# Delta rule: output norm and gate once for all chunks behind the convolutions, sums of squares on ScalarE, first mask folded into the decay

## The chip, the cores and the metric

The kernel runs on one core of a Trainium2 chip. The metric is device time in microseconds of one execution of the whole program. The engines are named as the profile names them: PE (matmuls), DVE (vector), ACT (activations), POOL (a second, slower elementwise engine), SP (which issues most DMAs).

## The reference, cut to what matters

The program is a stack of four blocks over 512 tokens of width 1024. The change touches only the first block, in which three branches are computed from one projection of the normed input and merged:

```python
def gated_delta_rule(q, k, v, g, beta):          # 4 heads of 128, chunk by chunk
    g = jnp.cumsum(g, axis=-1)
    ...
    lhs = a_kk + jnp.eye(CHUNK)                  # a_kk: strictly lower, k_beta k^T times decay
    sol = lax.linalg.triangular_solve(lhs, rhs, left_side=True, lower=True, unit_diagonal=True)
    ...
    def step(state, inp):
        v_new = u_c - w_c @ state
        o_c = q_c @ state + a_c @ v_new
        state = state * gl_c + k_c^T @ v_new

def gdn_branch(qkv, gate, a, b, conv_w, a_log, dt_bias, norm_w):
    q, k, v = split(silu(conv(qkv)))
    q = l2_normalize(q) * 128 ** -0.5            # x * rsqrt(sum(x*x) + EPS), per head
    k = l2_normalize(k)
    ...
    o = gated_delta_rule(q, k, v, g, beta)
    o = o * rsqrt(mean(o * o, axis=-1) + EPS) * norm_w     # per head
    return o * silu(gate)

y_a = gdn_branch(...)
y_b = stick_breaking_branch(sb_qkv)
y_c = short_conv_branch(sc_x, sc_b, sc_c, conv_sc_w)       # B * conv3(C * x)
merged = gate0 * (y_a @ w0) + gate1 * (y_b @ w1) + gate2 * (y_c @ w2)
```

## The kernel before, in words

A float32 matrix product is made of three matmuls of split operands (`h,whi`, `h,wlo`): `dense` makes one 128x512 block from 8 steps of 3 matmuls, 24 in all, in a PSUM bank `ps_d`. There are three `ps_d` banks, four `ps_p` banks for the delta rule's products and one `ps_s` bank for its state. Weights come through a stream: a DMA loads `wraw`, ACT makes `whi`, DVE makes `wlo`.

The delta rule (`gdn_core`) works on four chunks of 128 tokens. For each chunk `gdn_chunk_prep` turns k and q into token order on PE (transposes of `qkv` tiles at L534), sums their squares (ACT squares `sq`, DVE reduces into `qk_m`), takes a reciprocal root in some ten tiny DVE instructions (`rq_y`, `rq_a`), scales (`kt`, `qt`), transposes back (`kT`, `qT`, L540), and multiplies k by k and q by k into `pa` and `pq`. `dA` holds the decay times beta; `dA<-ps_p,dA` makes the matrix A of it. The inverse of I + A is then built level by level: a mask `lmask` picks a part of A (on POOL), the first one as `L`, the later ones as `Al`; R is the transpose of L; then six levels follow, each of which is `R,Al` (four matmuls), `E` on DVE, `E,L` (four matmuls), and a copy to the new `R` on ACT, with L transposed on DVE. Each step of a level waits for the one before. `gdn_chunk_step` carries the state: `S,kT`, `X,R`, `vn,kd`, and the outputs `S,qd` with `vn,dT` into `ps_s`. At its end stands the norm of the outputs: square on ACT (`gsq`), reduce and reciprocal root on DVE (`go_m`), the product `on`, four transposes on PE (L681) and four multiplications by the gate into `ya`.

`gdn_core` prepares chunk c+1 before it steps chunk c, so the one's step lies beside the other's levels. Behind `gdn_core` comes `short_conv`: four times three dense blocks (`px`, `pc`, `pb`), whose results go through the four temporaries `t` into a tile `yc`; then `stick_breaking` with the blocks of `sb_vf`. The dense blocks of what comes later in the code fill PE while the delta rule waits. Which of them stand where is fixed when the program is built: a scheduler gives each engine a fixed list of instructions, and each engine works through its list in order and waits where an operand is late. A tile of a tag is taken from a ring of buffers (`slot`): the tag `y` has 8 (before: four `ya`, taken ahead of the first chunk, then four `yc`), the tag `x` has 8 (among them the four gates `sgate`), `t` has 4.

```python
        with self.phase("mix", dict(d=3, p=4, s=1), qkv=12, gl=12, gp=6, gm=6, gs=5, y=8, t=4, tg=1):
```

Of the kernel before, what the change touches and what calls it, by code (L numbers as in the profile page):

```python
# [12 lines left out]
ALU = mybir.AluOpType  # L13
AF = mybir.ActivationFunctionType
AX = mybir.AxisListType

P = 128
# [131 lines left out]
class Kern:  # L149
# [373 lines left out]
    def gdn_chunk_prep(self, c):  # L523

        nc, G = self.nc, self.gdn
        cs = slice(c * P, (c + 1) * P)
        H4 = [P, 4, P]
        v3 = lambda t: t.rearrange("p (h n) -> p h n", h=4)
# [26 lines left out]
        dA = self.slot("gp", name="dA")  # L555
        self.tt(v3(dA), v3(t1), self.mstrict.unsqueeze(1).to_broadcast(H4), ALU.add)
        self.act(dA, dA, AF.Exp, scale=-1.0)
        self.tt(v3(dA), v3(dA), bc(G["beta"]), ALU.mult)
        dT = self.slot("gl", name="dT")
        self.tt(v3(dT), v3(t1), self.minclT.unsqueeze(1).to_broadcast(H4), ALU.add)  # L560
        self.act(dT, dT, AF.Exp)
# [2 lines left out]
        ssq = self.tmp("qk_m", shape=(P, 8))  # L564
        for i, ps in enumerate((pk, pq)):
            sq = self.slot("gs", name="sq")
            self.act(sq, ps, AF.Square)
            nc.vector.tensor_reduce(out=ssq[:, 4 * i:4 * i + 4], in_=v3(sq), axis=AX.X, op=ALU.add)
        self.ts(ssq, ssq, EPS, ALU.add)
        y = self.rsqrt(ssq, (P, 8), "8")  # L570
        self.ts(y[:, 4:8], y[:, 4:8], P ** -0.5, ALU.mult)
# [16 lines left out]
        pa, pq = self.ps("p"), self.ps("p")  # L588
        for h in range(4):
            hs = slice(h * P, (h + 1) * P)  # L590
            self.mm(pa[:, hs], kT[:, hs], kT[:, hs])
            self.mm(pq[:, hs], kT[:, hs], qT[:, hs])
        A, aq = dA, dT
        self.tt(A, pa, dA, ALU.mult)
        self.tt(aq, pq, dT, ALU.mult)

        I4 = self.ident.unsqueeze(1).to_broadcast(H4)
        I2 = self.ident.unsqueeze(1).to_broadcast([P, 2, P])
        v2 = lambda t: t.rearrange("p (h n) -> p h n", h=2)
        mk = lambda l: self.lmask[l - 1].unsqueeze(1).to_broadcast(H4)  # L600
        L = self.slot("gm", name="L")
        self.tt(v3(L), v3(A), mk(1), ALU.mult, nc.gpsimd)
        self.tt(v3(L), I4, v3(L), ALU.subtract)
        R = self.slot("gm", name="R")
        self.nc.vector.transpose(out=R, in_=L)
        for l in range(2, N_LEVELS + 1):
# [3 lines left out]
            R2 = self.slot("gl" if l == N_LEVELS else "gm", name="R")  # L610
            L2 = self.slot("gm", name="L") if l < N_LEVELS else None
            half = [slice(g * 2 * P, g * 2 * P + 2 * P) for g in range(2)]
# [10 lines left out]
            for g, c_ in enumerate(half):  # L623
                self.act(R2[:, c_], product(L, E, g))
                if l < N_LEVELS:
                    if l <= 5:
                        self.nc.vector.transpose(out=L2[:, c_], in_=R2[:, c_])
                    else:
                        nc.vector.tensor_copy(out=L2[:, c_], in_=product(E, L, g))
            L, R = L2, R2  # L630
        return dict(kT=kT, kd=kd, qd=qd, vb=vb, aq=aq, R=R, gl=gl)

    def gdn_chunk_step(self, c, w, S):

        nc, G = self.nc, self.gdn
        H4 = [P, 4, P]
        v3 = lambda t: t.rearrange("p (h n) -> p h n", h=4)
        hs = [slice(h * P, (h + 1) * P) for h in range(4)]
        if S is not None:
            pk = self.ps("s")  # L640
            for h in range(4):
                self.mm(pk[:, hs[h]], w["kT"][:, hs[h]], S[:, hs[h]])
            X = self.slot("gs", name="X")
            self.tt(v3(X), v3(pk), G["beg"][:, c, :].unsqueeze(2).to_broadcast(H4), ALU.mult)
            self.tt(X, w["vb"], X, ALU.subtract)
        else:
            X = w["vb"]
        pv = self.ps("s")
        for h in range(4):
            self.mm(pv[:, hs[h]], w["R"][:, hs[h]], X[:, hs[h]])  # L650
        vn = self.slot("gs", name="vn")
        self.act(vn, pv)
        S2 = None
        if c < 3:
            pS = self.ps("s")
            for h in range(4):
                self.mm(pS[:, hs[h]], w["kd"][:, hs[h]], vn[:, hs[h]])
            S2 = self.slot("gs", name="S")
            if S is None:
                self.act(S2, pS)  # L660
            else:
                Sg = self.slot("gs", name="Sg")
                self.tt(v3(Sg), v3(S), w["gl"].unsqueeze(2).to_broadcast(H4), ALU.mult, nc.gpsimd)
                self.tt(S2, pS, Sg, ALU.add)
        po = self.ps("s")
        for h in range(4):
            if S is not None:
                self.mm(po[:, hs[h]], w["qd"][:, hs[h]], S[:, hs[h]], stop=False)
            self.mm(po[:, hs[h]], w["aq"][:, hs[h]], vn[:, hs[h]], start=(S is None))

        sq = self.slot("tg", name="gsq")
        self.act(sq, po, AF.Square)
        m = self.tmp("go_m", shape=(P, 4))
        nc.vector.tensor_reduce(out=m, in_=v3(sq), axis=AX.X, op=ALU.add)
        self.ts(m, m, 1.0 / P, ALU.mult, EPS, ALU.add)
        ro = self.rsqrt(m, (P, 4))
        on = self.slot("gs", name="on")
        self.tt(v3(on), v3(po), ro.unsqueeze(2).to_broadcast(H4), ALU.mult)
        pt = self.ps("s")
        for h in range(4):  # L680
            nc.tensor.transpose(pt[:, hs[h]], on[:, hs[h]], self.ident)  # L681
        cs = slice(c * P, (c + 1) * P)
        for h in range(4):
            self.stt(self.ya[h][:, cs], pt[:, hs[h]], self.col("gdn_norm"), self.sgate[h][:, cs],
                     ALU.mult, ALU.mult)
        return S2

    def gdn_gate(self):
        self.sgate = []
# [9 lines left out]
    def gdn_core(self):  # L699
        lm = [self.slot("x", name="lmask") for _ in range(2)]  # L700
        for i in range(2):
            n = min(4, N_LEVELS - 4 * i) * P
            self.nc.scalar.dma_start(out=lm[i][:, 0:n], in_=self.ins["lmask"][:, i * T:i * T + n])
        self.lmask = [lm[i // 4][:, (i % 4) * P:(i % 4 + 1) * P] for i in range(N_LEVELS)]
        self.ya = [self.slot("y", name="ya") for _ in range(4)]
        S, w = None, self.gdn_chunk_prep(0)
        for c in range(4):
            nxt = self.gdn_chunk_prep(c + 1) if c < 3 else None
            S = self.gdn_chunk_step(c, w, S)
            w = nxt  # L710
# [1028 lines left out]
    def build(self):  # L1739
        self.load_constants()  # L1740
        with self.phase("mix", dict(d=3, p=4, s=1), qkv=12, gl=12, gp=6, gm=6, gs=5, y=8, t=4, tg=1):
            self.mark("norm0")
            self.first_norm()
            self.mark("gdn_proj")
            self.gdn_project()
            self.gdn_gate()
            self.gdn_decay()
            self.mark("gdn_core")
            self.gdn_core()
            self.mark("sc")  # L1750
            self.short_conv()
            self.mark("sb")
            self.stick_breaking(self.gates())
            self.dump_blocks("ya", self.ya)
            self.dump_blocks("yb", self.yb)
            self.dump_blocks("yc", self.yc)
            self.mark("merge")
            wo, accs, old = self.merge()
            self.mark("post0")
            x, hs = self.post_norm(wo, accs, "norm_mix_post", old, "norm_ffn_pre", keep=False, warm=(10, 8))  # L1760
            self.dump_blocks("x1", x)
        with self.phase("ffn1", dict(d=4, p=2, s=2), f=16, part=8, t=3, sy=7, sz=7, so=2):
            self.mark("ffn1")
            x, hs = self.ffn_relu2(x, hs, "norm_ffn_post", "mix0", self.s5_prepare())
            self.dump_blocks("x2", x)
        with self.phase("s5", dict(d=5, b=1, s=1), ut=3, U=5, matB=2, matE=3, matC=2, matL=2, w=6, rf=2, zz=4, half=8, t=4):
            self.mark("s5")
            x = self.s5_layer(x, hs)
            self.dump_blocks("x3", x)
        with self.phase("ffn2", dict(d=6, s=2), f=22, t=8):  # L1770
            self.mark("ffn2")
            x = self.ffn_swiglu(0, x, "ffn0")
            self.dump_blocks("x4", x)
        with self.phase("mla", dict(d=2, z=2, p=3, s=1), c=10, v=4, os=4, mp=7, pt=8, tm=3, t=4):
            self.mark("mla")
            x = self.mla(x)
            self.dump_blocks("x5", x)
            self.pad(self.sp, 96)
        with self.phase("ffn3", dict(d=6, s=2), f=22, t=8):
            self.mark("ffn3")  # L1780
            self.ffn_swiglu(1, x, "ffn1", last=True)
# [126 lines left out]
```

## Time and profile before

| | |
|---|---|
| median of 3 runs | 2231.46 us (2230.91 to 2231.72) |
| the profiled execution | 2235.85 us, span 2234.1 us |
| granted clock of TensorE, mean | 0.987 |
| busy: PE, DVE, ACT, POOL | 2160.5, 1361.5, 1005.8, 177.4 us |
| the delta rule's stretch of the span | about 113 to 282 us |

The profiled execution takes 4.39 us more than the median, 1.75 us of which lie outside its span. [...] PE is busy in 97% of the span, so what changes its waits and its clock changes the time.

### The profile page before, as it was taken

The numbers are of one execution on the slowest core, as the hardware profiler recorded it, in microseconds if no ns is written. First come the engines' busy times: TensorE is split into PE (matmuls) and PEld (weight loads), VectorE is DVE, ScalarE is ACT, GpSimd is POOL, SyncE is SP. The second block draws the span as 40 slices with busy tenths as digits, with TensorE's granted clock in tenths as the row PEclk, the third lists the DMA queues.
The fourth block names the chain that finished last, engine by engine and source line by source line (L and its number), as shares of the span: only waits on it lengthen the run. The fifth ranks groups of instructions, "written<-read, shape, count | busy, mean of one in ns | idle before, by whom it ended". The sixth has DMA issues, their size and how long they took to land.

```text
span 2234.1 us, 28560 instructions
## 1 busy us (share of the span) xinstructions
PE 2160.5 (97%) x10618; PEld 1794.2 (80%) x10618; DVE 1361.5 (61%) x2569; ACT 1005.8 (45%) x1926; POOL 177.4 (8%) x228
## 2 busy tenths in 40 slices
PE   8998999999999999999879999999999999999999
PEld 7777878888888888888668788888878877888887
DVE  6668756667658656666895554354477665543542
ACT  4443335666445454464224433233368765332331
POOL 4123200112000000000000000000022220000000
PEclk9999999999999999999989999999999999999999
DMA  4210123234523344343763223323221112233222
GB/s 153 90 48 29 43 80 119 95 114 156 174 67 105 125 150 141 132 155 103 237 212 124 85 95 101 97 95 95 92 72 34 48 38 66 95 101 98 95 95 94
DMA packets 83370, 231.57 MB, mean 104 GB/s; under 512 B 9632, under 2 KB 19360, under 8 KB 83232
## 3 DMA queue, kind: packets, MB, share of 16 engines
q1 hardware_dynamic: 74016, 208.60, 28.7%
q10 hardware_dynamic: 9216, 21.16, 2.9%
q8 instruction: 83, 1.36, 0.2%
q14 instruction: 55, 0.45, 0.1%
HBM read 202.46 MB, written 27.26 MB: 103 GB/s over the span
## 4 chain that ended last, share of the span: by engine, by line
PE 84%; DVE 9%; ACT 2%; issue 2%; DMA 2%; POOL 1%; SPq 0%; ACTq 0%; DVEq 0%; POOLq 0%
PE ps_d L250 71%; PE ps_p L282 3%; PE ps_z L250 2%; PE ps_p L250 1%; PE ps_s L1724 1%; DMA s5u<-ut 1%; PE ps_p L1699 1%; PE ps_s L282 1%; DVE wlo L224 1%; PE ps_p L1654 1%; DVE t L224 1%; PE ps_p L868 1%; DVE h L231 1%; DVE s5t L224 1%; ACT sb_e L234 1%
## 5 line engine op out<-in xcount | busy, mean ns | idle before, releaser
L250 PE MATMUL ps_d<-h,whi 128*128 128x512 f32 (+1 forms) x3184 | 1004.9, 393 | 8.9 <-DVE t L224 5.1
L234 ACT ACTIVATE whi<-wraw 128x512 fp32r<-128x512 f32 (+1 forms) x648 | 403.1, 625 | 716.8 <-PE ps_d L250 672.9
L250 PEld LDWEIGHTS ps_d<-h,whi 128*128 128x128 f32 (+1 forms) x3184 | 597.9, 189 | 135.0 <-ACT whi L234 4.0
L224 DVE TENSOR_TENSOR wlo<-wraw,whi 128x512 fp32r<-128x512 f32 x585 | 405.7, 697 | 383.6 <-ACT whi L234 378.1
L250 PE MATMUL ps_d<-h,wlo 128*128 128x512 f32 (+1 forms) x1592 | 626.4, 393 | 4.9 <-DVE wlo L224 4.9
L250 PEld LDWEIGHTS ps_d<-h,wlo 128*128 128x128 f32 (+1 forms) x1592 | 300.3, 189 | 67.6 <-DVE wlo L224 6.6
L250 PE MATMUL ps_d<-fh,whi 128*128 128x512 f32 x608 | 237.3, 390 | 0.0
L250 PE MATMUL ps_d<-fl,whi 128*128 128x512 f32 x608 | 237.0, 390 | 0.0
L250 PE MATMUL ps_d<-fh,wlo 128*128 128x512 f32 x608 | 236.6, 389 | 0.0
L224 DVE TENSOR_TENSOR t<-ps_d,rsb 128x512 f32<-128x512 f32 x136 | 92.9, 688 | 127.2 <-PE ps_d L250 124.3
L250 PEld LDWEIGHTS ps_d<-fl,whi 128*128 128x128 f32 x608 | 114.2, 188 | 23.7
L250 PEld LDWEIGHTS ps_d<-fh,wlo 128*128 128x128 f32 x608 | 114.2, 188 | 23.5
L250 PEld LDWEIGHTS ps_d<-fh,whi 128*128 128x128 f32 x608 | 114.2, 188 | 23.2
L224 POOL TENSOR_TENSOR wlo<-wraw,whi 128x512 fp32r<-128x512 f32 (+3 forms) x63 | 82.4, 1313 | 150.5 <-ACT whi L234 150.4
L234 ACT ACTIVATE fh<-t 128x512 fp32r<-128x512 f32 x76 | 47.9, 631 | 63.1 <-DVE t L224 54.4
L224 DVE TENSOR_TENSOR fl<-t,fh 128x512 fp32r<-128x512 f32 x76 | 52.5, 691 | 32.7 <-ACT fh L234 30.7
L250 PE MATMUL ps_d<-whi,c 128*128 128x256 f32 (+1 forms) x224 | 52.3, 318 | 2.9 <-ACT v L234 2.2
L224 DVE TENSOR_TENSOR x<-ps_d,x 128x512 f32<-128x512 f32 x56 | 38.6, 689 | 24.7 <-PE ps_d L250 24.4
L250 PE MATMUL ps_d<-zh,wlo 128*128 128x512 f32 x128 | 50.5, 394 | 0.9 <-DVE wlo L224 0.9
L250 PE MATMUL ps_d<-zh,whi 128*128 128x512 f32 x128 | 49.7, 401 | 1.5 <-ACT zh L234 0.9
L250 PE MATMUL ps_d<-zl,whi 128*128 128x512 f32 x128 | 49.8, 390 | 0.0
L224 DVE TENSOR_TENSOR acc<-acc,t 128x512 f32<-128x512 f32 x57 | 44.5, 780 | 4.6 <-ACT t L234 3.2
(391 smaller groups left out, 2911.5 us busy)
## 6 DMA issues: line engine op xcount, KB each, us to landing
wraw<-in_w_gu SPq DMA_DIRECT2D x88, 512.0 KB, 3.3
wraw<-in_w_ff SPq DMA_DIRECT2D x64, 512.0 KB, 3.3
wraw<-in_w_dn SPq DMA_DIRECT2D x44, 512.0 KB, 3.4
wraw<-in_w_gates SPq DMA_DIRECT2D x24, 512.0 KB, 3.4
wraw<-in_w_glu SPq DMA_DIRECT2D x16, 512.0 KB, 3.3
wraw<-in_w_sc SPq DMA_DIRECT2D x12, 512.0 KB, 3.4
gsc<-t SPq DMA_DIRECT2D x24, 256.0 KB, 2.0
sg<-gsc SPq DMA_DIRECT2D x24, 256.0 KB, 3.5
```

The lines of the kernel that those rows point to most:

```text
L224: self.note((eng or self.nc.vector).tensor_tensor(out=out, in0=a, in1=b, op=op))
L231: (eng or self.nc.vector).scalar_tensor_tensor(out=out, in0=a, scalar=s, in1=b, op0=op0, op1=op1)
L234: self.note(self.nc.scalar.activation(out, a, fn, **kw))
L250: self.note(self.nc.tensor.matmul(ps, lhsT=a, rhs=b, start=(start and n == 0), stop=(stop and n == 3 * len(ops) - 1), skip_group_check=loose))
L282: self.nc.tensor.matmul(ps, lhsT=lhsT, rhs=rhs, start=start, stop=stop)
L868: self.nc.tensor.matmul(self.sb_at(z, i), lhsT=self.tri if j == i else self.neg, rhs=self.sb_at(s, j), start=False, stop=(j == i and n == ...
L1654: self.nc.tensor.transpose(pt[:96, c * P:(c + 1) * P], src[:, c, l, :], self.ident)
L1699: self.nc.tensor.transpose(pt[:, oo:oo + P], p[bi][:, c0 + j * P:c0 + (j + 1) * P], self.ident)
L1724: self.note(nc.tensor.matmul(po[64 * h:64 * h + 64, 0:256], lhsT=V[j][:, head:head + 64], rhs=pt[h][j // 2][:, j % 2 * 256:j % 2 * 256 + 256],
```

## The change

Three things. The first mask is multiplied into the decay before the product `pa` is there (POOL `L<-dA,lmask` moves ahead of the transposed k; a DVE multiplication `L<-pa,L` takes its place behind `pa`). The sums of squares of k and q are taken by ACT itself, in eight squares of 128x128 with an accumulated output instead of two of 128x512 and two reduces on DVE. And the outputs are only copied from PSUM in each chunk (`yraw`, a tile of the tag `y`); squares, root, transposes and gate are done once for all four chunks in `gdn_finish`, which is called behind `short_conv` and writes into the gate's own tiles.

```diff
@@ gdn_chunk_prep
         self.tt(v3(dA), v3(dA), bc(G["beta"]), ALU.mult)
+        mk = lambda l: self.lmask[l - 1].unsqueeze(1).to_broadcast(H4)
+        L = self.slot("gm", name="L")
+        self.tt(v3(L), v3(dA), mk(1), ALU.mult, nc.gpsimd)
...
             sq = self.slot("gs", name="sq")
-            self.act(sq, ps, AF.Square)
-            nc.vector.tensor_reduce(out=ssq[:, 4 * i:4 * i + 4], in_=v3(sq), axis=AX.X, op=ALU.add)
+            for h in range(4):
+                self.act(sq[:, h * P:(h + 1) * P], ps[:, h * P:(h + 1) * P], AF.Square,
+                         accum_out=ssq[:, 4 * i + h:4 * i + h + 1])
...
         A, aq = dA, dT
+        self.tt(L, pa, L, ALU.mult)
         self.tt(A, pa, dA, ALU.mult)
         self.tt(aq, pq, dT, ALU.mult)
...
-        L = self.slot("gm", name="L")
-        self.tt(v3(L), v3(A), mk(1), ALU.mult, nc.gpsimd)
         self.tt(v3(L), I4, v3(L), ALU.subtract)
@@ gdn_chunk_step
+        y = self.slot("y", name="yraw")
+        self.act(y, po)
+        self.yraw.append(y)
+        return S2
+
+    def gdn_finish(self):
+
+        m = self.tmp("go_m", shape=(P, 16))
         sq = self.slot("tg", name="gsq")
-        self.act(sq, po, AF.Square)
-        m = self.tmp("go_m", shape=(P, 4))
-        nc.vector.tensor_reduce(out=m, in_=v3(sq), axis=AX.X, op=ALU.add)
+        hs = [slice(h * P, (h + 1) * P) for h in range(4)]
+        for c in range(4):
+            for h in range(4):
+                self.act(sq[:, hs[h]], self.yraw[c][:, hs[h]], AF.Square, accum_out=m[:, 4 * c + h:4 * c + h + 1])
         self.ts(m, m, 1.0 / P, ALU.mult, EPS, ALU.add)
-        ro = self.rsqrt(m, (P, 4))
-        on = self.slot("gs", name="on")
-        self.tt(v3(on), v3(po), ro.unsqueeze(2).to_broadcast(H4), ALU.mult)
-        pt = self.ps("s")
+        ro = self.rsqrt(m, (P, 16), "o")
+        for c in range(4):
+            v = self.yraw[c].rearrange("p (h n) -> p h n", h=4)
+            self.tt(v, v, ro[:, 4 * c:4 * c + 4].unsqueeze(2).to_broadcast([P, 4, P]), ALU.mult)
         for h in range(4):
-            nc.tensor.transpose(pt[:, hs[h]], on[:, hs[h]], self.ident)
-        cs = slice(c * P, (c + 1) * P)
-        for h in range(4):
-            self.stt(self.ya[h][:, cs], pt[:, hs[h]], self.col("gdn_norm"), self.sgate[h][:, cs],
-                     ALU.mult, ALU.mult)
-        return S2
+            pt = self.ps("s")
+            for c in range(4):
+                self.nc.tensor.transpose(pt[:, hs[c]], self.yraw[c][:, hs[h]], self.ident)
+            self.stt(self.sgate[h], pt, self.col("gdn_norm"), self.sgate[h], ALU.mult, ALU.mult)
+        self.ya = self.sgate
@@ gdn_core
-        self.ya = [self.slot("y", name="ya") for _ in range(4)]
+        self.yraw = []
@@ build
             self.short_conv()
+            self.gdn_finish()
```

The change also moves instructions in the engines' lists. The first place is PE's list in the levels of the last chunk. Before, dense matmuls (L250) stand between the level's steps:

```order
L282 MATMUL ps_p<-R,Al 128x128 x4
L250 MATMUL ps_d<-h,whi 128x512
L282 MATMUL ps_p<-E,L 128x128 x4
L250 MATMUL ps_d<-h,wlo 128x512
L250 MATMUL ps_d<-h,whi 128x512 x2
L282 MATMUL ps_p<-R,Al 128x128 x4
L250 MATMUL ps_d<-h,wlo 128x512
L250 MATMUL ps_d<-h,whi 128x512 x2
L250 MATMUL ps_d<-h,wlo 128x512
L282 MATMUL ps_p<-E,L 128x128 x4
```

In the changed program the last levels and the step behind them stand in PE's list without a dense matmul, as all six levels of this chunk do:

```order
L282 MATMUL ps_p<-R,Al 128x128 x4
L282 MATMUL ps_p<-E,L 128x128 x2
L282 MATMUL ps_p<-L,E 128x128 x2
L282 MATMUL ps_p<-E,L 128x128 x2
L282 MATMUL ps_p<-L,E 128x128 x2
L282 MATMUL ps_p<-R,Al 128x128 x4
L282 MATMUL ps_p<-E,L 128x128 x4
L282 MATMUL ps_s<-X,R 128x128 x4
```

The first dense matmul behind them, with the semaphores that each waits for, stands right behind the chunk's last output products and waits for DVE:

```order
L282 MATMUL ps_s<-S,qd 128x128
L282 MATMUL ps_s<-vn,dT 128x128
L250 MATMUL ps_d<-h,whi 128x512 [waits DVE_49]
L250 MATMUL ps_d<-h,wlo 128x512
L250 MATMUL ps_d<-h,whi 128x512 x2
```

What moved: 61 dense matmuls that stood ahead of this point now stand behind it; the three blocks that are complete by then lie in the three `ps_d` banks.

The second place is the short convolution's own work on ACT. Before, its first instruction on a `yc` stands between the levels of the second chunk:

```order
L234 ACTIVATE qT<-ps_p 128x512 [waits PE_49,Pool_49]
L234 ACTIVATE whi<-wraw 128x512 [waits PE_49]
L234 ACTIVATE yc<-t,cols 128x512
L234 ACTIVATE R<-ps_p 128x256 [waits PE_49,Activation_49]
L234 ACTIVATE R<-ps_p 128x256 [waits PE_49]
```

In the changed program the first two stand behind the last chunk's `yraw`:

```order
L234 ACTIVATE R<-ps_p 128x256 [waits PE_49] x3
L234 ACTIVATE vn<-ps_s 128x512 [waits PE_49,Pool_49]
L234 ACTIVATE yraw<-ps_s 128x512 [waits PE_49]
L234 ACTIVATE yc<-t,cols 128x512 x2
L234 ACTIVATE gsq,go_m<-yraw 128x128 [waits Activation_49]
```

And DVE's list has the rest of these two convolutions behind the last level, ahead of the instruction that empties a `ps_d` bank (`t<-ps_d`):

```order
L224 TENSOR_TENSOR E<-cst,ps_p 128x256 [waits PE_49]
L231 SCALAR_TENSOR_TENSOR yc<-t,cols,yc 128x511 [waits Activation_49] x2
L231 SCALAR_TENSOR_TENSOR yc<-t,cols,yc 128x510 [waits DVE_49] x2
L224 TENSOR_TENSOR yc<-yc,t 128x512 [waits DVE_49] x2
L224 TENSOR_TENSOR t<-ps_d,rsb_2039 128x512
L228 TENSOR_SCALAR go_m<-go_m 128x16 [waits Activation_49]
```

The four `yc` are taken from the ring of the tag `y` behind the fourth `yraw`, which is taken in the last chunk's step; before, the four `ya` were taken ahead of the first chunk.

## Rows read from the trace of the kernel before

**Rows 1.** The page's chain that ended last: share of the span by engine.
```profile
PE 84%; DVE 9%; ACT 2%; issue 2%; DMA 2%; POOL 1%; SPq 0%; ACTq 0%; DVEq 0%; POOLq 0%
```

**Rows 2.** PE's waits, 100 to 318 us: total, times, longest, in us.
```profile
PE ps_p L282 <- DVE go_m L228: 3.7, 2, 1.9
PE ps_p L282 <- DVE R L605: 3.4, 2, 1.8
```

**Rows 3.** Stretches of the delta rule: length, busy time of each engine, PEclk, DMA.
```profile
119.59:138.76 19.17, 16.53 (x91) 13.50 (x89) 14.71 (x33) 7.95 (x15) 4.84 (x4) 1.00 0.17 55
157.09:176.05 18.96, 15.98 (x101) 13.36 (x100) 17.33 (x42) 8.01 (x15) 4.85 (x4) 1.00 0.09 29
197.02:216.44 19.42, 17.29 (x109) 14.39 (x107) 16.78 (x35) 7.44 (x14) 5.89 (x5) 1.00 0.09 28
236.58:256.68 20.10, 17.80 (x113) 15.00 (x112) 16.24 (x35) 6.92 (x13) 5.90 (x5) 1.00 0.08 27
138.76:157.09 18.33, 18.33 (x134) 16.87 (x135) 10.71 (x25) 5.25 (x13) 6.73 (x5) 1.00 0.10 30
176.05:197.02 20.97, 20.25 (x146) 18.01 (x146) 17.89 (x36) 6.49 (x15) 6.55 (x5) 1.00 0.17 51
216.44:236.58 20.14, 19.89 (x137) 18.25 (x138) 15.50 (x41) 5.86 (x14) 6.36 (x5) 0.92 0.09 27
256.68:281.70 25.02, 24.68 (x169) 22.35 (x170) 19.59 (x46) 7.83 (x17) 6.37 (x5) 0.93 0.18 54
281.70:317.58 35.88, 35.64 (x159) 29.20 (x159) 16.47 (x35) 8.19 (x13) 0.00 (x0) 1.00 0.28 89
```

**Rows 4.** Timeline of the last chunk's first matrices: start, length, engine, instruction, idle before.
```profile
251.46 0.69 DVE L224 TENSOR_TENSOR dA<-ps_p,dA 128x512 f32<-128x512 f32 x1 [1.22 <-PE ps_p L282]
...
252.23 1.30 POOL L224 TENSOR_TENSOR L<-dA,lmask 128x512 f32<-128x512 f32 x1 [1.12 <-DVE dA L224]
...
253.48 1.29 POOL L224 TENSOR_TENSOR Al<-dA,lmask 128x512 f32<-128x512 f32 x1
...
253.56 1.76 DVE L224 TENSOR_TENSOR L<-cst,L 128x512 f32<-128x512 f32 x1 [0.82 <-POOL L L224]
...
255.25 0.67 DVE L674 TENSOR_REDUCE go_m<-gsq 128x4 f32<-128x512 f32 x1
255.84 0.69 DVE L605 STREAM_TRANSPOSE R<-L 128x512 f32<-128x512 f32 x1
...
256.68 1.28 PE L282 MATMUL ps_p<-R,Al 128*128 128x128 f32 x8 [1.86 <-DVE go_m L228]
```

**Rows 5.** Timeline of one level of the first chunk, same columns.
```profile
142.24 1.05 PE L282 MATMUL ps_p<-R,Al 128*128 128x128 f32 x8
...
143.37 1.15 PE L282 MATMUL ps_p<-E,L 128*128 128x128 f32 x8
...
144.11 0.83 ACT L234 ACTIVATE R<-ps_p 128x256 f32<-128x256 f32 x2 [1.98 <-PE ps_p L282]
```

**Rows 6.** ACT: copies and squares in the delta rule by form, then one with an accumulator elsewhere (timeline).
```profile
L234 ACT ACTIVATE R<-ps_p 128x256 f32<-128x256 f32 x48 | 18.5, 385 | 59.9 <-PE ps_p L282 58.8
L234 ACT ACTIVATE sq<-ps_p 128x512 f32<-128x512 f32 x8 | 4.7, 587 | 2.9 <-PE ps_p L534 2.9
```
```profile
1683.29 0.40 ACT L234 ACTIVATE mp<-mp,a_mn 128x128 f32<-128x128 f32 x1
```

**Rows 7.** Short convolution's instructions by form, 112.8 to 318 us: count, busy, mean ns.
```profile
L234 ACT ACTIVATE yc<-t,cols 128x512 f32<-128x512 f32 x4 | 2.9, 719 | 2.8 <-DVE t L224 2.7
L231 DVE SCALAR_TENSOR_TENSOR yc<-t,cols,yc 128x510 f32<-128x510 f32 x4 | 2.9, 718 | 0.0
```

**Rows 8.** Stretches of 2 us around 1130; columns as in rows 3.
```profile
1130.00:1132.00 2.00, 0.00 (x0) 0.03 (x1) 2.00 (x4) 1.42 (x5) 0.00 (x0) 0.50 0.40 111
...
1136.00:1138.00 2.00, 2.00 (x10) 1.90 (x10) 2.00 (x2) 0.00 (x0) 0.00 (x0) 0.50 0.70 201
```

**Rows 9.** Timeline of PE in the stick-breaking stage.
```profile
538.59 0.39 PE L262 MATMUL ps_s<-sb_al,v 128*128 128x256 f32 x1 [1.50 <-DVE sb_al L224]
```

More of the change, by code (lines that the diff above doesn't have):

```diff
@@ L599, in gdn_chunk_prep @@
         v2 = lambda t: t.rearrange("p (h n) -> p h n", h=2)
-        mk = lambda l: self.lmask[l - 1].unsqueeze(1).to_broadcast(H4)
-        L = self.slot("gm", name="L")
-        self.tt(v3(L), v3(A), mk(1), ALU.mult, nc.gpsimd)
         self.tt(v3(L), I4, v3(L), ALU.subtract)
```

## The prediction

> **What bounds the kernel now.** The chain that ended last lies on PE for 84% of the span [rows 1], so a change counts where it alters PE's idle time or PE's clock; work on the other engines counts only through these. I therefore read PE's waits next. In the delta rule the largest are those for the first R of a chunk: four waits of 1.6 to 1.9 us, 7.1 us together [rows 2] (the rows name `go_m` for two of them, an instruction that shares DVE's queue with R; in [rows 4] it is R that PE's `R,Al` follows). Then I cut the stretch at each chunk's first transpose of k and at its first `R,Al` [rows 3]: the first four rows are the preparations up to R, the next four the levels (the last with the chunk's own step), the ninth the dense work behind the delta rule up to the first `sb_vf` transpose. The reader should see that preparation is PE-busy for only 85 to 90%, that levels without a step beside them (the fifth row) are PE-busy throughout, and that two level stretches have a granted clock of 0.92 and 0.93.
>
> Two prices of PE are needed. The ninth row holds 155 dense matmuls and four `on` transposes: 35.88 us less 0.24 idle and 0.45 for the transposes, over 155, is 0.227 us for one dense matmul. The fifth row holds 22 dense matmuls and 56 small products in 18.33 us without idle time: 0.24 us for a small product.
>
> **What the change removes.** PE's own work stays: as many products, 16 output transposes, as many dense matmuls. What can fall is waiting, and what matters is which dense matmuls remain to fill it.
>
> First mask. Before, from `dA<-ps_p,dA` to `R,Al` the chain of [rows 4] is DVE 251.46, POOL 252.23 to 253.53, DVE `L<-cst,L` 253.56 to 255.32, a reduce of `go_m` in between, R from 255.84, PE at 256.68: 5.2 us. `L<-cst,L` reads SBUF alone and takes 1.76 us; it ends 0.55 us behind POOL's `Al`, so I read it as held until POOL is done. After: `L<-pa,L`, `dA` and `dT` 0.60 us apart (as the reduce and R are), POOL's `Al` from 1.34 to 2.63, so `L<-cst,L` held to 3.2, R to 3.85, PE at 3.95. The gain is 1.3 us a chunk on this chain, not POOL's full step with the reduce, because the mask that now runs beside it still holds DVE.
>
> Sums of squares. Before, a 128x512 square takes 0.59 us [rows 6] and a reduce 0.67 [rows 4]. After, four 128x128 squares stand for each; none with an accumulator from PSUM is in the trace. The nearest row, from SBUF, has 0.40 [rows 6]; the lower bound goes on from 512 columns at 0.587 and 256 at 0.385 [rows 6] to 0.28 at 128, an estimate. I take 0.3, since the source in PSUM is nearest to these: eight cost 2.4 us on ACT where two cost 1.2, and two reduces (1.2 us) leave DVE. The path k to `kt` gains little: 0.5, 0.4, 0.25 and 0.7 us for the four chunks, as DVE's tiny root instructions start when ACT's last square is through, and POOL's `L<-dA,lmask` now runs just then. At 0.40 a square this falls by 0.9 us in sum.
>
> [...]
>
> Preparations together. k to `kt` as above (-1.85), and `kt` to `R,Al`: -0.75, -1.9, -0.95 and -1.4 us. The second is largest since the tiny root of `go_m` (ten instructions) no longer stands ahead of `dA`. Sum of the four: **-6.85 us**.
>
> Levels of chunks 0 to 2. Without norm and gate beside them the second and third stretch should go as the first does now: 18.33 us with 22 dense matmuls [rows 3]. The second will have 22, the third 19 and one product more. That is 18.65 and 18.2 against 20.97 and 20.14 (the latter at a granted clock of 0.92, some 1.6 us lost behind its wait for R): **-4.25**, and **-0.2** for the first, which has one dense matmul less.
>
> **What the change adds.** Last chunk's levels. The changed order has no dense matmul among them. The work is 64 products of 0.24 us, 15.4 us, but without filler the chain sets the pace: `R,Al` to `E,L` 1.13 us, 0.74 to the copy of R, 0.42 for its first half and 0.1 to the next `R,Al` [rows 5], 2.39 us a level. Six levels with the extra `L,E` products, X, R and the outputs come to 18.25 us against 25.02 [rows 3]: **-6.75**, nearly all of it the 28 dense matmuls that left (6.4).
>
> Behind it. Dense filling stopped early because three finished blocks sit in the three banks: the fourth `t` can only come free when a `yc` is written, and the `yc` come behind the last `yraw`. So 61 more dense matmuls stand here, 61 x 0.227 = **+13.9**, and 12 more transposes at 0.11, **+1.3**. And the first dense matmul waits, with PE empty, for a list that starts when the outputs are in PSUM: 0.66 us for `yraw` (a 512-wide ACT instruction, 0.59 [rows 6], and the handover), 0.72 for the first `yc` on ACT, then on DVE four multiply-adds, two products and `t<-ps_d` at about 0.65 each (0.72 alone [rows 7], 0.60 in a row [rows 4]): 5.9 us, **+5.9**. Queued behind that instruction on PE is all dense work of the convolutions and of `sb_vf`; nothing else can run. After a wait like this the clock is down: around 1130 us PE had been empty, and the granted clock stayed at 0.50 to 1138 [rows 8], some 6 us of work at half speed, 3 us lost; behind the two shorter waits it was 1.6 and 1.75 us (0.08 of 20.14 and 0.07 of 25.02 [rows 3]). I take **+2.3**, between 1.6 and 3. Short waits for the single `ps_s` bank in `gdn_finish`: **+0.3**.
>
> Later. The gate's tiles now live to the merge, so four of the eight `x` buffers stay taken where the first stick-breaking heads want theirs. PE already waits there, 1.50 us at 538.59 [rows 9]. I take **+1.0**, between 0.3 and 2.
>
> **Sum.** -6.85 - 4.25 - 0.2 - 6.75 + 13.9 + 1.3 + 5.9 + 2.3 + 0.3 + 1.0 = +6.65 us. On the profiled execution's 2235.85 us that is 2242.5; it lies 4.4 us above the median of the runs shown, on which the sum gives **2238.1 us**. Something like 0.2%, 4.5 us, is what a measurement of this kernel can tell from no change, so the forecast is slower, not by much. In short: the waits that the change aims at were filled or short, and the one that it makes has nothing to fill it.
>
> **Rivals.** *It cancels* (no change). What DVE does beside POOL may be held less than I grant, which gives up to 0.65 us a chunk (`L<-cst,L` freed, 3.95 down to 3.3), 2.6 in all, and the clock may lose only 1.6 behind the long wait: 6.65 - 2.6 - 0.7 = +3.35, **2234.8 us**. For it: two of the four waits for R left no loss of clock at all [rows 2, 3]. Against: `L<-cst,L` was held in [rows 4], and it meets the same `Al` now. It decides from 2.2 us of gain on.
>
> *The convolutions are not held* (faster). If the short convolution's work ran among the levels as before, dense matmuls would fill the last chunk, and neither the wait nor the half clock would come. Then the preparations and levels keep their -11.3, the last levels gain the 1.75 us of their lost clock, and later work costs 1: -12.05, **2219.4 us**. The lists of ACT and DVE speak against it; it needs `t<-ps_d` to be done before the last `yraw`, and the list has it behind six instructions that need that `yraw` past. What decides is where that instruction starts.
>
> *The clock falls earlier too* (slower still). The last chunk has no filler from `kt` on, and PE there idles about 1.3 us before R and 0.5 in each level. The waits of up to 1.8 us in the first two chunks left the clock at 1.00 in the levels behind them, the two of up to 1.9 did not [rows 2, 3]. If half clock lasts through three of these levels, each with 1.9 us of work, some 1.4 us a level are lost, and the long wait's loss is 3: 6.65 + 4.2 + 0.7 = 11.5 at the most, half of that beyond the forecast is **2240.5 to 2243 us**.
>
> **How the numbers follow.** Forecast (2236 to 2240.5) 0.48; cancels 0.28; clock 0.15; not held 0.09. The range takes in the cancelling case and the clock's, and leaves out the faster one: 2230.5 to 2245.5. Slower by over 0.2% is the forecast and the clock's case with a little of their edge gone to no change: 0.61; within 0.2% 0.30; faster 0.09.
>
> **What would show it.** Right: in the last chunk's levels, no L250 row on PE between the first `R,Al` and the last output product, at a period near 2.4 us; behind it a wait of some 6 us put down to DVE's `t`, and a clock of 0.50 for some 4 to 6 us; the four waits for R at most 1 us each, with chunk 2 at full clock. Wrong: a wait of under 3 us there, a clock that stays at 1.00 behind it, a path from k to `kt` that is longer than before (then the squares cost over 0.40, or POOL holds more of the root), or a difference behind 320 us that is over 2 us either way.

## The result and the profile after

The changed kernel takes 2248.12 us (median of 4 runs, 2242.35 to 2249.78) against 2231.59: ratio 1.0066, interval 1.0045 to 1.0087, slower. The forecast was slower by 6.65 us, to 2238.1, in a range of 2230.5 to 2245.5. Measured were 16.5 us by these medians and 14.7 by the ratio, some 15 us, and the time lies outside the range. The two profiled executions differ by less, 2240.6 against 2234.1 us of span, but they are not alike in clock: the changed one had a mean granted clock of 0.990, its other three runs 0.986, the one before 0.987. So the parts below are read within the profile, and the totals from the medians.

The page's chain that ended last, which answers to [rows 1], hardly moves:

```profile
PE 85%; DVE 8%; ACT 3%; issue 2%; DMA 1%; POOL 1%; SPq 0%; ACTq 0%; POOLq 0%; DVEq 0%
```

PE's waits from 100 to 330 us, which answer to [rows 2]:

```profile
PE ps_d L250 <- DVE t L224: 5.9, 1, 5.9
PE ps_p L540 <- DVE kt L224: 3.2, 4, 1.4
PE ps_p L282 <- DVE R L607: 2.5, 4, 1.0
...
PE ps_s L282 <- DVE X L224: 1.0, 2, 0.5
```

The waits for R fell from 7.1 to 2.5 us, those for `kt` rose from 0.8 to 3.2, and a new one of 5.9 us stands first. The stretches, cut at the same instructions as in [rows 3] (four preparations, four levels, the dense work behind the wait):

```profile
118.23:136.01 17.78, 15.82 (x88) 12.94 (x86) 14.19 (x31) 8.39 (x28) 4.88 (x4) 1.00 0.19 59
153.94:170.30 16.36, 15.07 (x100) 12.81 (x98) 13.62 (x28) 9.49 (x36) 4.89 (x4) 1.00 0.10 34
188.37:206.21 17.84, 15.99 (x106) 13.59 (x105) 15.98 (x31) 8.91 (x35) 6.36 (x5) 1.00 0.19 60
224.02:241.94 17.92, 15.51 (x103) 12.98 (x102) 15.50 (x31) 9.13 (x35) 6.32 (x5) 1.00 0.18 59
136.01:153.94 17.93, 17.93 (x134) 16.48 (x135) 11.67 (x25) 5.67 (x14) 6.36 (x5) 1.00 0.10 31
170.30:188.37 18.07, 18.07 (x135) 16.63 (x136) 11.59 (x25) 5.24 (x13) 6.38 (x5) 1.00 0.10 30
206.21:224.02 17.81, 17.81 (x134) 16.45 (x134) 10.31 (x23) 5.15 (x13) 6.38 (x5) 1.00 0.01 2
241.94:261.96 20.02, 17.68 (x128) 15.23 (x128) 10.88 (x24) 5.19 (x13) 6.34 (x5) 1.00 0.00 1
267.83:321.11 53.28, 53.28 (x232) 43.72 (x233) 28.76 (x51) 12.20 (x19) 0.00 (x0) 0.96 0.26 85
```

From the first k transpose to the `sb_vf` transposes these are 202.88 us against 197.99, +4.9 (the sum had +5.65 for this stretch). Between the eighth and the ninth row lie the 5.87 us in which PE stands still. The timeline there shows who holds it:

```profile
262.00 0.60 ACT L234 ACTIVATE yraw<-ps_s 128x512 f32<-128x512 f32 x1 [2.14 <-PE ps_s L282]
262.50 1.32 ACT L234 ACTIVATE yc<-t,cols 128x512 f32<-128x512 f32 x2
263.24 2.73 DVE L231 SCALAR_TENSOR_TENSOR yc<-t,cols,yc 128x511 f32<-128x511 f32 x4 [6.03 <-ACT yc L234]
...
265.89 1.28 DVE L224 TENSOR_TENSOR yc<-yc,t 128x512 f32<-128x512 f32 x2
267.10 0.68 DVE L224 TENSOR_TENSOR t<-ps_d,rsb 128x512 f32<-128x512 f32 x1
...
267.83 0.80 PE L250 MATMUL ps_d<-h,whi 128*128 128x512 f32 x1 [5.87 <-DVE t L224]
```

DVE had been idle for 6.03 us when its first `yc` came: the work was not too much, it was late. Stretches of 4 us around it (columns as in [rows 3]) show the clock:

```profile
262.00:266.00 4.00, 0.00 (x0) 0.00 (x0) 2.76 (x5) 2.98 (x11) 0.00 (x0) 0.96 0.00 0
266.00:270.00 4.00, 2.17 (x5) 1.78 (x6) 3.89 (x9) 0.72 (x1) 0.00 (x0) 0.50 0.00 0
270.00:274.00 4.00, 4.00 (x13) 3.13 (x13) 3.79 (x14) 0.63 (x1) 0.00 (x0) 0.68 0.00 0
```

The nine dense matmuls from 268.43 us on take 3.84 us, 0.43 us for one, the nine from 273.33 on 2.06, 0.23 for one. At 0.50 for 2.17 us of work and at 0.68 over 4, the loss is 1.1 + 1.3 = 2.4 us, an estimate from these shares (taken: 2.3).

So the stretch as a whole went as forecast, and the rest of the 15 us lies elsewhere. One view tells where to look: the tile `fh`, the moving operand of the feed-forward blocks from 700 us on, which the change does not touch (count, then shortest, median and longest time in ns; first before, then after):

```profile
L250 PE MATMUL ps_d<-fh,whi x608: 387/389/478, 703.4 to 2229.3; 128*128 128x512 f32 x152
```

```profile
L250 PE MATMUL ps_d<-fh,whi x608: 388/394/481, 707.2 to 2236.0; 128*128 128x512 f32 x152
```

### The profile page after: what moved, and what is told of

Its sections match the earlier page's. It is cut to its first block, busy times and chain, and to the rows that moved or that the text cites. A ratio compares the mean times of both kernels' runs of the same rounds, so it can differ in the third digit from the quotient of the medians.

```text
span 2240.6 us, 28610 instructions
## 1 busy us (share of the span) xinstructions
PE 2163.4 (97%) x10618; PEld 1790.7 (80%) x10618; DVE 1354.4 (60%) x2519; ACT 1013.4 (45%) x2014; POOL 177.3 (8%) x228
## 4 chain that ended last, share of the span: by engine, by line
PE 85%; DVE 8%; ACT 3%; issue 2%; DMA 1%; POOL 1%; SPq 0%; ACTq 0%; POOLq 0%; DVEq 0%
PE ps_d L250 72%; PE ps_p L282 3%; PE ps_z L250 2%; PE ps_p L250 1%; PE ps_s L1733 1%; PE ps_p L1708 1%; PE ps_s L282 1%; PE ps_p L1663 1%; PE ps_b L282 1%; DVE wlo L224 1%; PE ps_p L877 1%; ACT sb_e L234 1%; DMA s5u<-ut 0%; DVE h L231 0%; PE ps_s L262 0%
## 5 line engine op out<-in xcount | busy, mean ns | idle before, releaser
L250 PE MATMUL ps_d<-h,whi 128*128 128x512 f32 (+1 forms) x3184 | 1005.6, 394 | 15.2 <-DVE t L224 11.0
L250 PEld LDWEIGHTS ps_d<-h,whi 128*128 128x128 f32 (+1 forms) x3184 | 598.4, 189 | 142.3 <-DVE t L224 8.3
L250 PE MATMUL ps_d<-h,wlo 128*128 128x512 f32 (+1 forms) x1592 | 625.8, 393 | 5.2 <-DVE wlo L224 5.2
L250 PEld LDWEIGHTS ps_d<-h,wlo 128*128 128x128 f32 (+1 forms) x1592 | 300.4, 189 | 68.8 <-DVE wlo L224 7.3
L250 PE MATMUL ps_d<-fh,whi 128*128 128x512 f32 x608 | 240.0, 395 | 0.0
L250 PE MATMUL ps_d<-fl,whi 128*128 128x512 f32 x608 | 238.3, 392 | 0.0
L250 PE MATMUL ps_d<-fh,wlo 128*128 128x512 f32 x608 | 236.8, 389 | 0.0
L250 PEld LDWEIGHTS ps_d<-fl,whi 128*128 128x128 f32 x608 | 114.1, 188 | 26.3
L250 PEld LDWEIGHTS ps_d<-fh,wlo 128*128 128x128 f32 x608 | 114.2, 188 | 24.7
L250 PEld LDWEIGHTS ps_d<-fh,whi 128*128 128x128 f32 x608 | 114.3, 188 | 23.1
L250 PE MATMUL ps_d<-whi,c 128*128 128x256 f32 (+1 forms) x224 | 51.5, 314 | 3.1 <-ACT v L234 2.4
L250 PE MATMUL ps_d<-zh,whi 128*128 128x512 f32 x128 | 49.9, 403 | 1.6 <-DVE ut L224 1.1
L250 PE MATMUL ps_d<-zh,wlo 128*128 128x512 f32 x128 | 50.2, 392 | 1.1 <-DVE wlo L224 1.1
L250 PE MATMUL ps_d<-zl,whi 128*128 128x512 f32 x128 | 49.7, 390 | 0.0
L1692 POOL MEMSET mp<- 128x128 f32 x32 | 6.4, 205 | 512.6 <-PE ps_d L250 451.4
```

The costliest lines, as they stand in the source:

```text
L250: self.note(self.nc.tensor.matmul(ps, lhsT=a, rhs=b, start=(start and n == 0), stop=(stop and n == 3 * len(ops) - 1), skip_group_check=loose))
L1692: nc.gpsimd.memset(p[b][:, c0 + n:c0 + n + P], 0.0)
```

## The experiments

Two theories stood against each other. **A**: the wait behind the last chunk, and what it costs, is the whole loss. **B**: something beside the delta rule's stretch costs as much again.

### The changed kernel once more (e_after2)

No edit.

> The changed kernel once more, for a second profiled execution. Theory A (the wait behind the last chunk and what it costs is all): the stretch from the first k transpose to the sb_vf transposes is again 4 to 6 us longer than before (202 to 204 us against 197.99), and the median lies 5 to 8 us above before. Theory B (something beside that stretch costs as much again): the median is again 14 to 19 us above before, the stretch is the same, and the difference lies behind 320 us: a lower granted clock in stretches that the change did not touch, or dense matmuls that follow each other at a longer distance than 0.2275 us.

2248.21 us, ratio 1.0066 (1.0051 to 1.0081). In its profile the stretch is 202.83 us and the wait 5.87 again, and `fh,whi` has 394 ns again. Behind the stretch this profile is 6.9 us longer than before (1923.4 us against 1916.5), at a mean granted clock of 0.988 against 0.987. The stretch is as A says, the total as B.

### A ring of its own for the raw outputs (e_yr)

```diff
-        y = self.slot("y", name="yraw")
+        y = self.slot("yr", name="yraw")
-  ... gs=5, y=8, t=4, tg=1):
+  ... gs=5, y=4, yr=4, t=4, tg=1):
-            o = self.slot("y", name="wo")
+            o = self.slot("yr" if m < 4 else "y", name="wo")
```

> The raw outputs get a ring of four buffers of their own (and the ring of the convolutions shrinks to four), so that a convolution's tile no longer comes behind the last chunk's raw output; nothing else of the change is undone. Theory A: dense matmuls stand between the last chunk's levels again, the wait of 5.9 us for t is under 1 us, and the median falls to 2219 to 2227 us, 4 to 12 us faster than before. Theory B: the stretch gets shorter by 12 to 16 us, but the time stays above 2228 us, since half of the loss lies elsewhere.

2232.58 us, ratio 0.9995 (0.9985 to 1.0004) to before: 15.6 us below the changed kernel. The wait is gone, and in the list the `yc` stand among the levels again. That settles where the 5.9 us came from, but the time is not the 2219 to 2227 of theory A; it is B's. `fh,whi` has 394 ns here too. (The same four tiles asked for earlier in the code, in the old ring, give the same lists on all engines; this program was not timed.)

### The parts apart (e_mask_sq, e_finish, e_mask)

e_mask_sq is the kernel before with the change's first two hunks, e_mask with the mask alone; e_finish is the changed kernel without both.

> Only the mask and the sums of squares are changed, norm and gate of the outputs stand in each chunk as before. Theory A: shorter preparations and no held convolution: 3 to 8 us faster than before. Theory B, in its form that new small tiles shift later buffers and slow the matmuls: dense matmuls as fast as before (median 389 ns for fh,whi), since this kernel has no new tile; time 2224 to 2229 us.

> Only the norm and gate of the outputs are moved behind the convolutions; mask and sums of squares as before. Theory A: the held convolutions and the wait for t stay (5 to 6 us), the gains of the other two parts are missing: 10 to 16 us slower than before. Theory B in the form of shifted buffers: fh,whi at 394 ns as in the changed kernel, and 15 to 22 us slower than before.

> Only the first mask is folded into the decay. With the sums of squares beside it, the two parts gave 4.3 us. Theory M (the shorter chain to R carries that): 3 to 5 us faster than before, with the waits for R down from 1.6 to 1.9 us each to under 1 us in the first and the last two chunks. Theory S (the squares carry it): less than 1.5 us faster.

| | median us | before, same chip | ratio | `fh,whi` ns |
|---|---|---|---|---|
| e_mask | 2228.34 | 2233.46 | 0.998 (0.9971 to 0.999) | 389 |
| e_mask_sq | 2229.24 | 2233.59 | 0.9984 (0.9974 to 0.9993) | 389 |
| e_finish | 2248.7 | 2233.59 | 1.0071 (1.0054 to 1.0088) | 394 |

The mask gives some 5 us (in its profile PE waits 0.57 or 0.58 us for the first R in three chunks and 1.08 in the second), the squares beside it nothing that shows. All of the loss comes with the late norm, and with it come the 394 ns. The gains do not simply add: mask and squares together gain 4.4 us alone, but beside the late norm no more than 0.5 by the medians (2248.7 without them, 2248.21 with them). The stretches of the two profiles, 204.32 and 202.88 us with a wait of 5.87 us in both, agree; why so little is left is open.

### Shifted buffers alone (e_before_320, 64, 128, 256)

The late norm brings three small tiles of 16 columns in the pool of small tiles, two buffers each. They push every buffer of the later pools 320 bytes up in its partition. The kernel before, with nothing changed but the width of one small tile:

```diff
-        m = self.tmp("go_m", shape=(P, 4))
+        m = self.tmp("go_m", shape=(P, 44))[:, 0:4]      # 320 bytes; 16: 64, 24: 128, 40: 256
```

> The kernel before with nothing changed but the size of one small tile (go_m gets 44 columns, of which 4 are used), so that every buffer of the later pools lies 320 bytes further in its partition, as in the changed kernel; no instruction and no place in a list is different. Theory P (the place of the buffers makes dense matmuls slower): fh,whi at a median of 394 ns instead of 389, yh,whi too, and 4 to 5.5 us slower than before. Theory Q (what slows these matmuls is the late norm, by its tiles or its order): 389 ns and the same time as before.

> The kernel before with go_m of 16 columns: later buffers lie 64 bytes further, nothing else. If any shift off the old places costs (they lie at multiples of 512 bytes): fh,whi at 394 ns, some 5 to 7 us slower than before. If the cost needs a shift by a part of 128 or 256 bytes, it is there too; if it grows with the shift, about 390 ns and 1 to 2 us.

> The same with 40 columns: later buffers lie 256 bytes further. If what counts is a place at a multiple of 512 bytes: 394 ns, some 5 to 7 us slower than before. If a multiple of 256, 128 or 64 bytes is enough: 389 ns and the time of before.

> The kernel before with go_m of 24 columns: later buffers lie 128 bytes further, nothing else. A shift by 64 bytes cost 6 to 7 us, one by 256 bytes nothing. If a place at a multiple of 128 bytes is enough: fh,whi at 389 ns and the time of before. If it needs a multiple of 256: 394 ns and 5 to 7 us slower.

| shift, bytes | median us | before, same chip | ratio | `fh,whi`, `fh,wlo` ns |
|---|---|---|---|---|
| 64 | 2239.46 | 2233.46 | 1.0032 (1.0019 to 1.0045) | 394, 388 |
| 128 | 2247.26 | 2231.21 | 1.0069 (1.0049 to 1.0089), 2 runs | 394, 396 |
| 256 | 2232.63 | 2233.46 | 1.0 (0.9989 to 1.001) | 389, 389 |
| 320 | 2239.45 | 2232.95 | 1.0027 (1.0018 to 1.0037) | 394, 388 |

Not an instruction differs among these. The view of `fh` and `fl` (the second part of the split operand) in the kernel with 320 bytes, then of `fh` with 128 and with 256:

```profile
L250 PE MATMUL ps_d<-fh,whi x608: 388/394/481, 702.5 to 2234.6; 128*128 128x512 f32 x152
L250 PE MATMUL ps_d<-fl,whi x608: 388/392/481, 703.0 to 2235.1; 128*128 128x512 f32 x152
```

```profile
L250 PE MATMUL ps_d<-fh,whi x608: 387/394/482, 703.9 to 2241.6; 128*128 128x512 f32 x152
L250 PE MATMUL ps_d<-fh,wlo x608: 387/396/404, 704.1 to 2241.8; 128*128 128x512 f32 x152
```

```profile
L250 PE MATMUL ps_d<-fh,whi x608: 387/389/478, 701.4 to 2224.9; 128*128 128x512 f32 x152
L250 PE MATMUL ps_d<-fh,wlo x608: 387/389/397, 701.6 to 2225.1; 128*128 128x512 f32 x152
```

A few ns, then, on many of some two thousand matmuls, in a stage where PE is hardly ever idle (busy for 1491 of the 1529 us from 700 to 2229 in the kernel before): theory P of the expectations, and the form that B takes. In the profile with 320 bytes the three forms (`fh,whi`, `fh,wlo`, `fl,whi`) are busy for 715.1 us together, against 710.9 before: 4.2 of the 6.5 us by which that kernel's median is longer (4 to 5.5 were expected). Its delta rule's stretch is no longer than before (197.00 us against 197.99). With 128 bytes the three are busy for 721.7 us, and the loss, 16 us, is more than twice the 5 to 7 expected.

### Which buffer it is (e_f64, e_t64)

In the last two feed-forward blocks, e_f64 puts a small unused tile ahead of `fh` and `fl`, e_t64 one ahead of the temporaries (and one behind them, so that `fh` and `fl` move by 256).

```diff
+        t = self.pool.tile([P, n], F32, name="pad", tag=f"pad{n}", bufs=1)   # 16 columns, or 16 and 48
+        self.nc.gpsimd.memset(t, 0.0)
```

> The kernel before with a small unused tile (set to zero on POOL) between the temporaries and the tiles f of the last two feed-forward blocks: there fh and fl alone lie 64 bytes further, everything else where it was. If the place of the moving operand itself decides: fh,whi between 1300 and 2230 us at 394 ns, between 700 and 1030 us (first feed-forward block) at 389, and 1 to 3 us slower than before. If the place of other buffers decides: 389 ns everywhere.

> The mirror image: in the last two feed-forward blocks the temporaries t lie 64 bytes further, fh and fl 256 bytes further (a shift that cost nothing). If the place of the moving operand decides: 389 ns and the time of before. If the place of what DVE and ACT write and read beside it decides: 394 ns there and 1 to 3 us slower.

The view of `fh` from 1290 to 1620 us, first e_f64, then e_t64:

```profile
L250 PE MATMUL ps_d<-fh,whi x176: 394/394/397, 1374.3 to 1614.2; 128*128 128x512 f32 x176
```

```profile
L250 PE MATMUL ps_d<-fh,whi x176: 389/389/389, 1372.1 to 1610.8; 128*128 128x512 f32 x176
```

Outside the two blocks both have 389. So the place of the moving operand is enough, and that of the temporaries is not what counts. The 175 steps of this block take 239.9 us from first to last in the one and 238.7 in the other, 1.2 us a block, with no `fh,whi` over 397 ns in either; the medians, 1.0003 (0.9992 to 1.0014) and 1.0011 (0.9999 to 1.0022), can't tell 2.4 us.

### Both mends (e_after_al, e_yr_al) and the held x buffers (e_yr_gl_al, e_after_al_gl)

"al" puts the three small tiles into rings that exist, so that nothing moves; "gl" writes the gated outputs into the ring `gl`. (In e_yr_gl_al, and in e_best_nosq below, the four raw tiles are also asked for ahead of the first chunk.)

```diff
-        m = self.tmp("go_m", shape=(P, 16))
+        m = self.tmp("hs_m", shape=(P, 56))[:, 0:16]
-        ro = self.rsqrt(m, (P, 16), "o")
+        ro = self.rsqrt(m, (P, 16), "h")
...
-            self.stt(self.sgate[h], pt, self.col("gdn_norm"), self.sgate[h], ALU.mult, ALU.mult)
+            y = self.slot("gl", name="ya")                       # gl
+            self.stt(y, pt, self.col("gdn_norm"), self.sgate[h], ALU.mult, ALU.mult)
```

> The changed kernel with its three new small tiles put into rings that exist already, so that every later buffer lies where it lay before; the lists of all engines are those of the changed kernel. Theory P: fh,whi at 389 ns again, 4 to 5.5 us faster than the changed kernel, that is 9 to 12 us slower than before. Theory Q: 394 ns and some 15 us slower than before.

> Both mends together: the raw outputs in a ring of their own, and later buffers where they lay before. Theory P: the sum of the two, 4.5 to 7 us faster than before. Theory Q: as with the ring alone, within 2 us of before.

> As the kernel with both mends, and the gated outputs go into a ring that the delta rule has done with (gl) instead of the gate's own tiles, so that the gate's x buffers come free as before. If the held x buffers cost what I took (1.0 us, 0.3 to 2): 0.5 to 2 us faster than with the two mends alone, and the drift of 0.4 to 1 us between 530 and 545 us of the changed kernel is gone. If they cost nothing: the same within 0.5 us.

> The changed kernel with later buffers at their old places (some 6.7 us slower than before), and the gated outputs in the ring gl, so that the x buffers come free as before. If the held x buffers cost 2.5 us, as the profiles of the two kernels with a ring for the raw outputs have it: 3.5 to 5 us slower than before, and no wait of over 1.6 us at sb_al near 540 us. If they cost nothing: again 6 to 7 us slower.

| | median us | before, same chip | ratio |
|---|---|---|---|
| e_after_al | 2239.69 | 2232.95 | 1.0026 (1.0017 to 1.0036) |
| e_after_al_gl | 2238.84 | 2231.21 | 1.0039 (1.0025 to 1.0054) |
| e_yr_al | 2226.77 | 2232.95 | 0.9965 (0.9952 to 0.9979) |
| e_yr_gl_al | 2224.32 | 2232.95 | 0.9956 (0.9941 to 0.997) |

With the buffers at their old places (e_after_al) `fh,whi` takes 389 ns again:

```profile
L250 PE MATMUL ps_d<-fh,whi x608: 387/389/478, 709.7 to 2235.9; 128*128 128x512 f32 x152
```

The change then costs 6.7 us by the medians (9 to 12 were expected), which is the sum of the prediction. With both mends it is faster than before by 6.2 us, and with the third by 8.6, the fastest kernel here. The x buffers show in the waits near 540 us (e_after_al, then e_after_al_gl):

```profile
PE ps_s L262 <- DVE sb_al L224: 1.8, 1, 1.8
```

```profile
PE ps_s L262 <- DVE sb_al L224: 0.6, 1, 0.6
PE ps_s L262 <- ACT sb_ah L234: 0.5, 1, 0.5
```

The wait, 1.5 us in the kernel before [rows 9], shrinks, but in time the pairs disagree (2.5 us less with the ring for the raw outputs, intervals that overlap; no gain without it). What the held x buffers cost is not settled.

### Without the squares on ACT (e_best_nosq)

e_yr_gl_al with the sums of squares of k and q as before, on ACT and DVE.

> The kernel with both mends and the gated outputs in the ring gl, but with the sums of squares of k and q on ACT and DVE as before. Where the squares stand on ACT, PE waits 1.4 us for kt in the first chunk and 0.8 us in the last. Theory M: these waits shrink, and the time is 0.5 to 3 us below that of the kernel with the squares on ACT. Theory S: the reduces on DVE come back ahead of kt, and it is 1 to 4 us slower than that.

2229.05 us, ratio 0.9979 (0.9968 to 0.9989), against 0.9956 (0.9941 to 0.997) with them. The times lean to theory S, but the intervals overlap by a little, so they do not settle it. The profiles lean the same way: without the squares on ACT the stretch is 191.80 us, with them 188.67, and in the first chunk PE goes from k to its first transpose of `kt` in 11.02 us against 9.48, with the two reduces in DVE's list ahead of `kt`. Beside the mask alone (e_mask_sq) the squares gained nothing.

## Why the prediction was wrong, point by point

**The step that failed** is the one sentence that no term stands for: "PE's own work stays: as many products, 16 output transposes, as many dense matmuls", and with it the inference that behind 320 us only the held x buffers could cost anything. The count stays, the duration does not. The changed program's small tiles move the operands of later matmuls by 320 bytes, `fh,whi` takes 394 instead of 389 ns, and this shift alone, put on the kernel before, costs 6.5 us. The diff shows the three tiles, and the kernel before pads its pool of small tiles ahead of the last block (`self.pad(self.sp, 96)`); I read neither as a matter of time. Taken out of the changed kernel, the same shift is worth 7.9 us: 14.6 us of loss with it (e_after2), 6.7 without (e_after_al). The 6.5 and the 7.9 agree within the spread of the runs. One of the prediction's signs of being wrong, a difference of over 2 us behind 320 us, is there: 6.9 us in e_after2.

**The rest of the sum held, in part by errors that cancel.** Preparations: 77.65 to 69.90 us, -7.75 (-6.85). Of this, k to PE's first transpose of `kt` gave -3.4 (-1.85), although PE's waits for `kt` grew, and from there to `R,Al` -4.4 (-5.0). Levels of chunks 0 to 2: -0.40, -2.90 and -2.33, together -5.6 (-4.45). Last levels: 25.02 to 20.02, -5.0 (-6.75): the pace was 2.6 to 2.8 us a level, not 2.39, since PE waits for POOL's `Al` ahead of three of the levels, and in the slowest one for `E`:

```profile
244.54 1.16 PE L282 MATMUL ps_p<-R,Al 128*128 128x128 f32 x8 [0.24 <-POOL Al L224]
246.07 1.16 PE L282 MATMUL ps_p<-E,L 128*128 128x128 f32 x8 [0.38 <-DVE E L224]
247.35 1.13 PE L282 MATMUL ps_p<-R,Al 128*128 128x128 f32 x8
```

Behind it: 59.15 us with the wait against 35.88, +23.3 (13.9 + 1.3 + 5.9 + 2.3 + 0.3 = +23.7). The wait was 5.87 us (5.9). These four parts miss their terms by -0.9, -1.2, +1.75 and -0.4 us. That e_after_al comes out at the sum's 6.7 us is therefore partly luck, and the +1.0 for the held x buffers is not settled.

**The first mask** went as [rows 4] let one expect. In the last chunk:

```profile
237.80 0.69 DVE L224 TENSOR_TENSOR L<-ps_p,L 128x512 f32<-128x512 f32 x1 [1.22 <-PE ps_p L282]
...
239.23 1.27 POOL L224 TENSOR_TENSOR Al<-dA,lmask 128x512 f32<-128x512 f32 x1 [1.78 <-DVE dA L224]
...
239.60 1.45 DVE L224 TENSOR_TENSOR L<-cst,L 128x512 f32<-128x512 f32 x1
...
241.94 0.79 PE L282 MATMUL ps_p<-R,Al 128*128 128x128 f32 x5 [0.32 <-DVE R L607]
```

4.14 us from the first to the last (3.95). `L<-cst,L` took 1.45 us, where two `yc<-yc,t` of the same width, with POOL idle, took 1.28 together (at 265.89 above); and it ended some 0.55 us behind POOL's `Al`, here as in the other three chunks and in all four of the kernel before. So I read it as held until POOL is done, as taken; without the hold it would have been over by 240.3, an estimate from the 0.69 of `L<-ps_p,L`.

**The squares** were near the low bound:

```profile
154.57 0.28 ACT L234 ACTIVATE sq<-ps_p 128x128 f32<-128x128 f32 x1 [0.95 <-PE ps_p L534]
154.75 0.19 ACT L234 ACTIVATION_READ_ACCUMULATOR sq<-ps_p 128x1 f32 x1
154.84 0.27 ACT L234 ACTIVATE sq<-ps_p 128x128 f32<-128x128 f32 x1
```

0.27 us from one to the next; over all 32 of the profile, 0.26 to 0.30 for one, with a median of 0.276 (taken: 0.3; low bound 0.28, an estimate).

**The rivals.** "It cancels" is not what happened: with the shift taken out, the interval of e_after_al lies above no change. "The convolutions are not held" is refuted by the 5.87 us, and e_yr shows its mechanism from the other side. Its price was too high: it was given 12.05 us, and with the ring and the buffers at their old places the kernel is 6.2 us faster, 8.6 without the held x buffers too. "The clock falls earlier too" did not come: 1.00 in all four levels of the profiled execution. None of the rivals held a loss outside the stretch.

## What to carry to other kernels

In a kernel whose PE is hardly ever idle (here busy in 97% of the span), compare the median time of one matmul form in a stage that the change does not touch: 5 ns there were worth about as much here as the wait that was looked for. The new small tiles did that here, so look where such a tile puts the buffers behind it. And a tile moved behind a later stage holds everything that takes from the same ring: here four convolution tiles waited for the last raw output, and the filler of PE with them, which a ring of its own cured (15.6 us; 12.9 with the buffers at their old places).

## What the runs showed of the hardware that was not expected

- Dense float32 matmuls with a 128x512 moving operand took 389 ns where that operand lay at its place in the kernel before, a multiple of 512 bytes in its partition, or 256 bytes past it (medians of `fh` and `fl`). At 64 and 320 bytes past it `fh,whi` took 394, `fl,whi` 392 and `fh,wlo` 388; at 128 they took 394, 397 and 396. In e_f64 `fh` and `fl` alone moved, by 64 bytes, and `fh,whi` took 394: the moving operand's own place was enough. It is not the whole story: in the kernel with 320 bytes `ybh,whi` also rose, from 389 to 397, though `ybh` had not moved; in that stage its matmuls stand, in groups, between those of `yh`, which had. Why is open.
- Runs of the same program differed, and their times went roughly with the mean granted clock: ten runs of e_yr go from 2229.92 us at 0.991 to 2235.86 at 0.986. The changed kernel's run at 0.990 was 5.4 to 7.4 us shorter than its three at 0.986, so the spans of two profiled executions at 0.987 and 0.990 can't be compared to a few us.
